# Twenty more warm-up products, wider buffers in a ring of weights, and the low parts of all weights on VectorE

## The chip, the core and the metric

The kernel runs on one core of a Trainium2 chip. The core has a matrix engine (TensorE, PE in the rows, with its weight loads as PEld), a vector engine (VectorE, DVE), an activation engine (ScalarE, ACT), a general engine (GpSimd, POOL) and a queue engine that issues most transfers (SyncE, SP). They run side by side and wait for one another through semaphores. The metric is the device time of one execution in microseconds; the time of a kernel is the median of its runs.

## What is computed

One decoder block on a sequence of 1024 tokens of width 1024, all in float32. A conditioning vector gives shift, scale and gate; a combined input projection feeds a pooling mixer and a chunked state-space (SSD) mixer; an output projection and a squared-ReLU MLP follow:

```python
mod = einsum('bd,de->be', silu(c), w_ada) + b_ada          # six vectors: shift, scale, gate, twice
u = rms_norm(h, g_mix) * (1 + scale_m) + shift_m
proj = einsum('bsd,de->bse', u, w_in)                      # pool | z | x,B,C | dt
y_pool = pool_mixer(proj[..., :OFF_Z], w_pool, pool_scale)
y_ssd = ssd_mixer(z, u_xbc, u_dt, ...)                     # causal conv, silu, chunked scan, gate by silu(z), norm
h = h + gate_m * einsum('bse,ed->bsd', concat(y_pool, y_ssd), w_out)
u = rms_norm(h, g_mlp) * (1 + scale_f) + shift_f
f = square(relu(einsum('bsd,df->bsf', u, w_up)))
h = h + gate_f * einsum('bsf,fd->bsd', f, w_down)
return rms_norm(h, g_final)
```

## The kernel before

Each large product of two float32 matrices is done as three products of a reduced 32-bit format (fp32r): an operand is split into a high part `hi`, a rounded copy made by ScalarE (line 195), and a low part `lo`, which is operand minus `hi` (line 196). `mm3` (line 238) then issues hi·hi, hi·lo and lo·hi on TensorE; line 245 is its one matmul, so nearly all matmuls of the profile have that line.

The work comes in stages. Stage 1, the start: x is loaded, normalized by rows, transposed on TensorE (line 139) and scaled by the first shift and scale vectors, which are themselves products of the conditioning vector with pieces of `w_ada` (partly on VectorE, lines 441 to 443 and 265 to 267, partly on TensorE, lines 450, 368, 370 and 464). Eight steps (`chunk`, line 483) then accumulate six 128x512 results. Until the first step can begin, `busy(n)` (line 332) issues plain float32 products whose result nobody reads: 7 after the first transpose, and 2 at a time between the early pieces of work. In this stage the order on ScalarE, VectorE, GpSimd and TensorE is the written one (`pinned`). Stage 2 (about 72 to 330 us): the other columns of the input projection. `feat` (line 601) makes 128 channels for 512 tokens with 24 matmuls; `conv_half` (line 551) takes the result through a copy to `craw` (ACT), a small copy of three columns (POOL, lines 558, 560), one activation (line 562), three multiply-adds on VectorE (line 565), a tanh (line 568) and a last multiply (line 573 or 576); a transpose of the result on TensorE follows 12 us of planned time later (line 583). The short `dec` steps on VectorE (lines 641 to 653) turn the step sizes dt of the scan, and the scan itself is mixed in. Stage 3 (to 540 us): the z columns, the norm, and the output projection `gemm2` (line 967), where the weights are the moving operand. Stage 4 (to the end): the MLP, whose operands lie in other buffers (`dhi`, `dlo`, `whl`).

Weights of stages 2 and 3, and of the first products of the MLP, pass through a ring: `unit` (line 184) loads a piece to `raw`, and splits it to `hi` and `lo`. The ring's six `hi` and six `lo` buffers have 544 floats, that is 2176 bytes a partition, and lie one behind the other. In the built program the six `hi` buffers begin at bytes 203200, 205376, 207552 and so on, the `lo` buffers at 216256, 218432 and so on: by turns 192 and 64 bytes past a multiple of 256. The pieces take the buffers in turn. The other operands of the matmuls (`u`, `ym`, `dhi`, `dlo`, `whl`) all begin 192 past such a multiple. The ring of stage 1 has 768 floats a buffer.

`ring["pool_lo"]` says which engine makes `lo`: GpSimd for the 15 pieces asked for between line 529 and line 780, VectorE for all others. Outside the pinned stage the order of each engine's instructions is set by the framework's scheduler from the program and its own costs. `z_tok` (line 884) gates with z: a tanh to `th`, a product to `sz`, a product to `tok`.

Of the kernel before, what the change touches and what calls it, by code (L numbers as in the profile page):

```python
# [9 lines left out]
F32 = mybir.dt.float32  # L10
F32R = mybir.dt.float32r
BF16 = mybir.dt.bfloat16
AF = mybir.ActivationFunctionType
ALU = mybir.AluOpType
# [3 lines left out]
P = 128  # L18
# [16 lines left out]
NFG = DFF // HW  # L35
EPS = 1e-5
UM = 544
WARM = 7
CUTS = (0, 0, 0, 2, 4, 4, 0)
TDVE = (1, 2, 3)  # L40
AP = (4, 1, 1, 1, 1, 1, 1)
# [29 lines left out]
def tile_hybrid_block(  # L71
# [112 lines left out]
    def unit(kn, ncol, parts, gate=None):  # L184
        n = kn * ncol
        rp, hp, w, rb, hb = ring["now"]
        raw = rp.tile([P, w], F32, name="raw", tag="raw" if w == UM else "raws", bufs=rb)
        rv = raw[:, :n].rearrange("p (k c) -> p k c", c=ncol)
        for c0, c1, src in parts:
            sp.dma_start(out=rv[:, :, c0:c1], in_=src)  # L190
        if gate is not None:
            dve.tensor_tensor(out=rv, in0=rv, in1=gate.unsqueeze(1).broadcast_to([P, kn, ncol]), op=ALU.mult)
        hi = hp.tile([P, w], F32R, name="hi", tag="hi", bufs=hb)
        lo = hp.tile([P, w], F32R, name="lo", tag="lo", bufs=hb)
        act.copy(hi[:, :n], raw[:, :n])  # L195
        (pool if ring.get("pool_lo") else dve).tensor_tensor(  # L196
            out=lo[:, :n], in0=raw[:, :n], in1=hi[:, :n].bitcast(F32), op=ALU.subtract)
        hv = hi[:, :n].rearrange("p (k c) -> p k c", c=ncol)
        lv = lo[:, :n].rearrange("p (k c) -> p k c", c=ncol)
        return [(hv[:, k, :], lv[:, k, :]) for k in range(kn)]  # L200
# [118 lines left out]
    def row_rs(t, eng=dve):  # L319
        square_sum(t, slice(0, D), t, utmp().bitcast(BF16))  # L320
        rsqrt_cols(t, t + 1, D, eng)
# [9 lines left out]

    def busy(n):
        for _ in range(n):
            pe.matmul(warm_ps[:, 0:P], lhsT=ident, rhs=ones, start=True, stop=True)  # L334

    def transpose_x(k, h, ps):
        for i in range(4):
# [68 lines left out]
    ring["now"] = (stp, stp, 768, 2, 2)  # L406
    kw = []
    with pinned((act, dve, pool, pe)):
        row_rs(0)
        row_scale(0, False)  # L410
        row_rs(1)
        pst = bank()
        turn(pst[:, 0:P], pr0[:, :])
        busy(WARM)
        dve.tensor_copy(out=pc[:, 0:64], in_=pst[:, 0:64])
        dve.tensor_scalar(out=chf, in0=pc[:, 0:8], scalar1=0.5, scalar2=None, op0=ALU.mult)
        row_scale(1, False)
        row_rs(2)
        act.activation(out=cth, in_=pc[:, 0:8], func=AF.Tanh, scale=0.5)
        dve.scalar_tensor_tensor(out=cact, in0=cth, scalar=1.0, in1=chf, op0=ALU.add, op1=ALU.mult)  # L420
        for j in (8, 32):
            sl = pc[:, C_BADA + j:C_BADA + j + 8]
            dve.tensor_scalar(out=sl, in0=sl, scalar1=1.0, scalar2=None, op0=ALU.add)
        row_scale(2, False, slice(0, HW))
        row_rs(3)
        row_scale(2, True, slice(HW, D))
        spec = specs.popleft()
        raw0 = stp.tile([P, 768], F32, name="raw", tag="raws", bufs=2)
        for c0, c1, src in spec[2]:
            sp.dma_start(out=raw0[:, c0:c1].unsqueeze(1), in_=src)  # L430
        ada_load(0)
        acc = [stp.tile([P, 256], F32, name="adaa", tag="adaa", bufs=4)[:, :P] for _ in range(2)]
        hi0 = stp.tile([P, 768], F32R, name="hi", tag="hi", bufs=2)
        lo0 = stp.tile([P, 768], F32R, name="lo", tag="lo", bufs=2)

        def dve_f0(ks):
            for k in ks:
                a = acc[k % 2]
                src = ada_w[0][:, k, 0:P]
                if k < 2:  # L440
                    dve.tensor_scalar(out=a, in0=src, scalar1=cact[:, k:k + 1], scalar2=None, op0=ALU.mult)
                else:
                    dve.scalar_tensor_tensor(out=a, in0=src, scalar=cact[:, k:k + 1], in1=a,
                                             op0=ALU.mult, op1=ALU.add)

        pa, pb = bank()[:, 0:1], bank()[:, 0:1]

        def pe_f1(ks):
            for k in ks:
                pe.matmul(pb, lhsT=ada_w[0][:, k, P:2 * P], rhs=cact[:, k:k + 1], start=k == 0, stop=k == KD - 1)  # L450

        act.copy(hi0, raw0)
        dve_f0(range(2))
        row_scale(3, False, slice(0, HW))
        row_scale(3, True, slice(HW, D))
        dve_f0(range(2, KD))
        dve.tensor_tensor(out=lo0, in0=raw0, in1=hi0.bitcast(F32), op=ALU.subtract)
        for i in range(3):
            pe_f1(range(2 * i, 2 * i + 2))
            busy(2)  # L460
        stage_x(0)
        pe_f1(range(6, KD))
        for i in range(2):
            pe.matmul(pa, lhsT=acc[i], rhs=ones[:, 0:1], start=i == 0, stop=i == 1)
        ada_cols(0, pa, pb)
        ada_u(0)
        stage_x(1)
        busy(WARM2)
        kw.append([(hi0, lo0)])
        ada_load(1)  # L470
        pool.dma_start(out=pr1[0:48, :], in_=conv_w[0].rearrange("k (r p) -> (k r) p", p=P))
        pool.dma_start(out=pr1[48:60, :], in_=rows(conv_b))
        pool.dma_start(out=pr1[64:72, :], in_=rows(g_mlp))
        pool.dma_start(out=pr1[72:80, :], in_=rows(g_ssd))
        pool.dma_start(out=pr1[80:84, :], in_=rows(pool_scale))
        pool.dma_start(out=dtb, in_=dt_bias.broadcast_to([P, HEADS]))
        pool.dma_start(out=nea, in_=a_log.broadcast_to([P, HEADS]))
        pool.dma_start(out=dsk, in_=d_skip.broadcast_to([P, HEADS]))
# [4 lines left out]
    def chunk(k):  # L483
# [22 lines left out]
            kw.append(get(1, 0))  # L506
        if k == 5:
            ring["now"] = (unitm, unitm, UM, 4, 6)
            ring["pool_lo"] = False
            for i in range(4):  # L510
                specs.append((2, 256, [
                    (0, Z0, win_r[:, 2 * i:2 * i + 2, OFF_Z:OFF_Z + Z0]),
                    (Z0, 256, win_r[:, 2 * i:2 * i + 2, OFF_DT:OFF_DT + HEADS])], None))
            feat_specs(G1[0][0])
            prefetch(NPF)
# [10 lines left out]
    chunk(6)  # L526
    chunk(7)
    prefetch(6)
    ring["pool_lo"] = True
    st.close()  # L530
    for off, _ in G0 + G1[1:]:
        feat_specs(off)
# [244 lines left out]
    for _, ct in G0:  # L777
        conv_half(ct, 1, feat(get(2, 3), 1))
        step(5.2)
    ring["pool_lo"] = False  # L780
    queue_ssd(0)
    for i, (_, ct) in enumerate(G1[1:]):
        ks = get(2, 3)
# [100 lines left out]
    def z_tok(si, t, ks):  # L884
# [3 lines left out]
        tok_mm(ps[:, :n], t, ks)  # L888
        th = accp.tile([P, 272], F32, name="zt", tag="zt", bufs=2)
        act.activation(out=th[:, :n], in_=ps[:, :n], func=AF.Tanh, scale=0.5)  # L890
        sz = accp.tile([P, 272], F32, name="sz", tag="sz", bufs=2)
        dve.scalar_tensor_tensor(out=sz[:, :n], in0=th[:, :n], scalar=1.0, in1=ps[:, :n],
                                 op0=ALU.add, op1=ALU.mult)
        dve.scalar_tensor_tensor(out=tok[:, t, a:b], in0=tok[:, t, a:b], scalar=0.5, in1=sz[:, :n],
                                 op0=ALU.mult, op1=ALU.mult)
        if si != 1:
            g = 0 if si == 0 else 1
# [652 lines left out]
```

## Time and profile before

| | |
|---|---|
| median of 3 runs | 1170.3 us (1166.7 to 1172.98) |
| the profiled execution | 1170.18 us |
| its span, first to last instruction | 1168.3 us |
| busy: PE, DVE, ACT, POOL | 1143.4 (98%), 823.9 (71%), 561.8 (48%), 169.7 us (15%) |
| 15 `lo` on POOL, mean | 1.46 us each, 100.4 to 147.5 us |
| mean granted TensorE clock | 0.997 of 2.4 GHz |

TensorE is busy nearly all the span, so time is lost where it waits, where it runs at its lower clock, or where one product takes longer than another of the same size. A matmul's row shows its own duration, which overlaps the next; the rate is read from the distance between starts. The clock column has no record before the first change of the clock, and shows 1.00 there; the durations tell which level it was. A float32 product appears as two matmul records, an fp32r product or a transpose as one.

### The profile page before, as it was taken

Reading aid. Unit: us, or ns where it says so; the run is one execution under the profiler, and the core shown is the slowest. Engines: PE = TensorE matmul, PEld = TensorE weight load, DVE = VectorE, ACT = ScalarE, POOL = GpSimd, SP = SyncE. Lnnn points to the kernel's source line nnn. Section 1 sums busy time; section 2 is a strip of 40 time slices with the busy share of each in tenths; the row PEclk is TensorE's granted clock in tenths of the full one; section 3 lists DMA queues with packets and bytes.
Section 4 is the critical chain, followed back from the end, with each engine's and each line's share of the span. In section 5 each row is a group of like instructions: output and inputs, shape, how many; then the busy total and the mean of one; then the engine's idle time right before and its main releaser. Section 6 shows DMA issues by size and latency. Waiting matters only on the chain.

```text
span 1168.3 us, 15472 instructions
## 1 busy us (share of the span) xinstructions
PE 1143.4 (98%) x5639; PEld 953.8 (82%) x5639; DVE 823.9 (71%) x1220; ACT 561.8 (48%) x981; POOL 169.7 (15%) x204
## 2 busy tenths in 40 slices
PE   7999999999999999999999999999999999999997
PEld 6888787777799888887778888888888888888885
DVE  3878789967978656664888666665567844586985
ACT  4476575544434633534764444444354344334373
POOL 3014436514500011122000000000100000000030
PEclk9999999999999999999999999999999999999999
DMA  9942233233367646753166434351499934775732
GB/s 260 241 137 61 68 129 106 72 86 114 100 197 226 205 140 201 259 162 126 37 212 220 151 147 170 128 189 72 154 399 358 320 110 144 238 262 186 270 127 90
DMA packets 124908, 200.73 MB, mean 172 GB/s; under 512 B 8448, under 2 KB 67616, under 8 KB 122784
## 3 DMA queue, kind: packets, MB, share of 16 engines
q1 hardware_dynamic: 123472, 196.24, 50.3%
q0 software_dynamic: 1120, 3.21, 0.8%
q8 instruction: 44, 0.72, 0.3%
q14 instruction: 32, 0.26, 0.1%
q10 hardware_dynamic: 240, 0.30, 0.1%
HBM read 159.81 MB, written 39.91 MB: 171 GB/s over the span
## 4 chain that ended last, share of the span: by engine, by line
PE 83%; DVE 8%; DMA 3%; ACT 3%; issue 2%; POOL 1%; POOLq 0%; SPq 0%; ACTq 0%; DVEq 0%
PE bank L245 74%; PE bank L743 2%; DMA raw<-in_w_ada_dram 2%; DVE cv L565 2%; PE bank L139 2%; PE bank L747 1%; PE bank L740 1%; DVE acc L851 1%; PE bank L334 1%; PE bank L819 1%; DVE lo L196 1%; ACT tok L905 1%; PE bank L1026 1%; POOL rst L180 0%; DMA adaa<-in_b_ada_dram 0%
## 5 line engine op out<-in xcount | busy, mean ns | idle before, releaser
L245 PE MATMUL bank<-u,hi 128*128 128x512 f32 x560 | 185.6, 411 | 0.4 <-ACT u L386 0.4
L245 PE MATMUL bank<-dhi 128*128 128x512 f32 (+1 forms) x452 | 175.1, 387 | 1.1 <-DVE tmp L1446 1.1
L245 PE MATMUL bank<-dlo,dhi 128*128 128x512 f32 (+1 forms) x452 | 175.0, 387 | 0.0
L245 PE MATMUL bank<-dhi,dlo 128*128 128x512 f32 (+1 forms) x452 | 175.0, 387 | 0.0
L1380 ACT CAST dhi<-fr 128x1024 fp32r<-128x1024 f32 x56 | 59.0, 1054 | 144.4 <-PE bank L245 110.5
L245 PEld LDWEIGHTS bank<-u,hi 128*128 128x128 f32 x560 | 104.6, 191 | 28.0 <-issue 5.0
L1381 DVE TENSOR_TENSOR dlo<-fr,dhi 128x1024 fp32r<-128x1024 f32 x56 | 68.5, 1224 | 83.3 <-ACT dhi L1380 83.0
L245 PE MATMUL bank<-hi,ym 128*128 128x512 f32 x384 | 125.4, 400 | 0.0
L195 ACT CAST hi<-raw 128x512 fp32r<-128x512 f32 (+2 forms) x109 | 67.9, 633 | 90.8 <-PE bank L245 70.1
L245 PE MATMUL bank<-u,lo 128*128 128x512 f32 x280 | 111.1, 397 | 0.0
L196 DVE TENSOR_TENSOR lo<-raw,hi 128x512 fp32r<-128x512 f32 (+2 forms) x94 | 72.2, 781 | 48.5 <-ACT hi L195 48.1
L245 PEld LDWEIGHTS bank<-dhi 128*128 128x128 f32 x452 | 84.9, 188 | 18.5 <-DVE tmp L1446 1.3
L245 PEld LDWEIGHTS bank<-dlo,dhi 128*128 128x128 f32 x452 | 84.9, 188 | 17.5
L245 PEld LDWEIGHTS bank<-dhi,dlo 128*128 128x128 f32 x452 | 84.9, 188 | 17.3
L245 PE MATMUL bank<-hi,u 128*128 128x256 f32 (+1 forms) x512 | 97.4, 288 | 0.2
L245 PE MATMUL bank<-E,whl 128*128 128x512 f32 x384 | 91.6, 389 | 0.0
L245 PEld LDWEIGHTS bank<-hi,ym 128*128 128x128 f32 x384 | 72.1, 188 | 16.4 <-issue 0.7
L180 POOL TENSOR_TENSOR rst<-ssq,mhalf 128x1 f32<-128x1 f32 (+2 forms) x27 | 26.9, 998 | 400.9 <-DVE ssq L179 375.8
L245 PEld LDWEIGHTS bank<-E,whl 128*128 128x128 f32 x384 | 72.1, 188 | 15.0
L245 PEld LDWEIGHTS bank<-hi,u 128*128 128x128 f32 x512 | 80.1, 189 | 1.4 <-issue 0.7
L245 PE MATMUL bank<-u,whl 128*128 128x512 f32 x312 | 75.2, 389 | 0.8 <-ACT whl L1160 0.8
L245 PE MATMUL bank<-lo,ym 128*128 128x512 f32 x192 | 75.4, 392 | 0.0
(257 smaller groups left out, 2144.6 us busy)
## 6 DMA issues: line engine op xcount, KB each, us to landing
f_d<-tok SPq DMA_DIRECT2D x16, 1792.0 KB, 7.3
wr<-in_w_down_dram SPq DMA_DIRECT2D x56, 512.0 KB, 5.0
fr<-f_d SPq DMA_DIRECT2D x53, 512.0 KB, 4.4
raw<-in_w_ada_dram SPq DMA_DIRECT2D x64, 256.0 KB, 3.1
wraw<-in_w_up_dram SPq DMA_DIRECT2D x16, 1024.0 KB, 5.4
raw<-in_w_in_dram SPq DMA_DIRECT2D x48, 256.0 KB, 3.0
raw<-in_w_out_dram SPq DMA_DIRECT2D x48, 256.0 KB, 2.8
tok<-in_x_dram SPq DMA_DIRECT2D x16, 512.0 KB, 6.1
```

Source lines behind the costliest of these rows:

```text
L139: return pe.transpose(dst, src, ident)
L180: pool.tensor_tensor(out=rst[:, a:b], in0=m, in1=mhalf[:, :b - a], op=ALU.pow)
L195: act.copy(hi[:, :n], raw[:, :n])
L196: (pool if ring.get("pool_lo") else dve).tensor_tensor(out=lo[:, :n], in0=raw[:, :n], in1=hi[:, :n].bitcast(F32), op=ALU.subtract)
L245: pe.matmul(ps, lhsT=st_, rhs=mv, start=first and i == 0, stop=last and i == 2, skip_group_check=more)
L334: pe.matmul(warm_ps[:, 0:P], lhsT=ident, rhs=ones, start=True, stop=True)
L565: dve.scalar_tensor_tensor(out=v, in0=cr[:, k:k + HW], scalar=pw[:, 12 * k + ct:12 * k + ct + 1], in1=v, op0=ALU.mult, op1=ALU.add)
L740: pe.matmul(po, lhsT=C[:, cs], rhs=states[g], start=True, stop=True)
L743: pe.matmul(py[:, hh * HD:(hh + 1) * HD], lhsT=Ms[hh // 4][:, (hh % 4) * P:(hh % 4 + 1) * P], rhs=xdt[:, hh * HD:(hh + 1) * HD], start=Tru ...
L747: pe.matmul(pst_, lhsT=btok, rhs=xw, start=True, stop=True)
L1380: act.copy(hi, src)
L1381: dve.tensor_tensor(out=lo, in0=src, in1=hi.bitcast(F32), op=ALU.subtract)
```

## The change

Twenty products are issued ahead of the first transpose. The products of `busy` take `ones` as both operands, where one was `ident` before (`ident` is made on GpSimd, `ones` by a memset on VectorE). The ring's `hi` and `lo` buffers get 576 floats (2304 bytes, 9 times 256) of which as many are used as before; in the built program all twelve then begin 192 past a multiple of 256. All `lo` are made on VectorE. `z_tok` overwrites `th` in place of using `sz`; the bytes of the two `sz` buffers go to the ring.

```diff
+UP = 576
 WARM = 7
+WARM0 = 20
...
-        hi = hp.tile([P, w], F32R, name="hi", tag="hi", bufs=hb)
-        lo = hp.tile([P, w], F32R, name="lo", tag="lo", bufs=hb)
+        hi = hp.tile([P, UP if w == UM else w], F32R, name="hi", tag="hi", bufs=hb)
+        lo = hp.tile([P, UP if w == UM else w], F32R, name="lo", tag="lo", bufs=hb)
         act.copy(hi[:, :n], raw[:, :n])
-        (pool if ring.get("pool_lo") else dve).tensor_tensor(
-            out=lo[:, :n], in0=raw[:, :n], in1=hi[:, :n].bitcast(F32), op=ALU.subtract)
+        dve.tensor_tensor(out=lo[:, :n], in0=raw[:, :n], in1=hi[:, :n].bitcast(F32), op=ALU.subtract)
...
-            pe.matmul(warm_ps[:, 0:P], lhsT=ident, rhs=ones, start=True, stop=True)
+            pe.matmul(warm_ps[:, 0:P], lhsT=ones, rhs=ones, start=True, stop=True)
...
     with pinned((act, dve, pool, pe)):
+        busy(WARM0)
         row_rs(0)
...
-            ring["pool_lo"] = False
...
-    ring["pool_lo"] = True
...
-    ring["pool_lo"] = False
...
-        sz = accp.tile([P, 272], F32, name="sz", tag="sz", bufs=2)
-        dve.scalar_tensor_tensor(out=sz[:, :n], in0=th[:, :n], scalar=1.0, in1=ps[:, :n],
+        dve.scalar_tensor_tensor(out=th[:, :n], in0=th[:, :n], scalar=1.0, in1=ps[:, :n],
                                  op0=ALU.add, op1=ALU.mult)
-        dve.scalar_tensor_tensor(out=tok[:, t, a:b], in0=tok[:, t, a:b], scalar=0.5, in1=sz[:, :n],
+        dve.scalar_tensor_tensor(out=tok[:, t, a:b], in0=tok[:, t, a:b], scalar=0.5, in1=th[:, :n],
```

The first rows of TensorE before. L139 is the first transpose, of the small parameters; L334 the products of `busy`; L450 the first shift products.

```order
L139 MATMUL bank<-ident,adaa 128x128
L334 MATMUL bank<-ones,ident 128x128 x7
L450 MATMUL bank<-cact,adaw 128x1 x2
L334 MATMUL bank<-ones,ident 128x128 x2
L450 MATMUL bank<-cact,adaw 128x1 x2
```

The same place after (lines have moved by one or two: L335 is `busy`, L141 the transpose).

```order
L335 MATMUL bank<-ones 128x128 x20
L141 MATMUL bank<-ident,adaa 128x128
L335 MATMUL bank<-ones 128x128 x7
L452 MATMUL bank<-cact,adaw 128x1 x2
L335 MATMUL bank<-ones 128x128 x2
L452 MATMUL bank<-cact,adaw 128x1 x2
```

The transpose stands behind the twenty; the rest of TensorE's order is the same to the end.

GpSimd in stage 2 before, from the last carry of the first half of a convolution on. L196 is a `lo`, L560 the small copy that a convolution's second half needs.

```order
L560 COPY craw<-car 128x3
L196 TENSOR_TENSOR lo<-raw,hi 128x512 x2
L560 COPY craw<-carry_782 128x3
L196 TENSOR_TENSOR lo<-raw,hi 128x512 x2
L560 COPY craw<-carry_783 128x3
L196 TENSOR_TENSOR lo<-raw,hi 128x512
L560 COPY craw<-carry_784 128x3
```

The same place after.

```order
L560 COPY craw<-car 128x3
L560 COPY craw<-carry_802 128x3
L560 COPY craw<-carry_803 128x3
L560 COPY craw<-carry_804 128x3
L560 COPY craw<-carry_805 128x3
```

No `lo` is left there.

VectorE in stage 2 before, up to the last multiply (L576, `cv_1449`) of the sixth of these convolutions, whose transpose follows on TensorE. L565 are multiply-adds of a convolution, L573 its last multiply where B or C channels are made, L698 a product of the scan, `bt` and `ct` are B and C.

```order
L573 SCALAR_TENSOR_TENSOR bt_835<-craw_1334,cv_1337 128x512
L698 TENSOR_TENSOR xdt_1742<-tok_66,dt_795 128x512
L698 TENSOR_TENSOR xdt_1819<-tok_66,dt_795 128x512
L565 SCALAR_TENSOR_TENSOR cv_1396<-craw_1393,pw_117,cv_1396 128x512 x3
L573 SCALAR_TENSOR_TENSOR ct_876<-craw_1393,cv_1396 128x512
L565 SCALAR_TENSOR_TENSOR cv_1449<-craw_1446,pw_117,cv_1449 128x512 x3
L576 SCALAR_TENSOR_TENSOR cv_1449<-craw_1446,cv_1449 128x512
```

The same place after (L198 is a `lo`; `cv_1469` is the tile that was `cv_1449`).

```order
L565 SCALAR_TENSOR_TENSOR cv_1416<-craw_1413,pw_117,cv_1416 128x512
L198 TENSOR_TENSOR lo_1485<-raw_1482,hi_1484 128x512
L198 TENSOR_TENSOR lo_1540<-raw_1537,hi_1539 128x512
L573 SCALAR_TENSOR_TENSOR ct_896<-craw_1413,cv_1416 128x512
L698 TENSOR_TENSOR xdt_1762<-tok_66,dt_815 128x512
L565 SCALAR_TENSOR_TENSOR cv_1469<-craw_1466,pw_117,cv_1469 128x512
L198 TENSOR_TENSOR lo_1546<-raw_1543,hi_1545 128x512
L565 SCALAR_TENSOR_TENSOR cv_1469<-craw_1466,pw_117,cv_1469 128x512
L698 TENSOR_TENSOR xdt_1839<-tok_66,dt_815 128x512
L565 SCALAR_TENSOR_TENSOR cv_1469<-craw_1466,pw_117,cv_1469 128x512
L198 TENSOR_TENSOR lo_1593<-raw_1590,hi_1592 128x512
L576 SCALAR_TENSOR_TENSOR cv_1469<-craw_1466,cv_1469 128x512
```

Four `lo` stand in these rows where none stood, between the last steps of two convolutions, and the two L698 are apart. Of the 15 `lo`, 14 stand ahead of this L576.

## Rows read from the trace of the kernel before

**Rows 1.** The page: busy time, share of the span and instructions of TensorE, and the chain that ended last by line.

```profile
PE 1143.4 (98%) x5639; PEld 953.8 (82%) x5639; DVE 823.9 (71%) x1220; ACT 561.8 (48%) x981; POOL 169.7 (15%) x204
...
PE bank L245 74%; PE bank L743 2%; DMA raw<-in_w_ada_dram 2%; DVE cv L565 2%; PE bank L139 2%; PE bank L747 1%; PE bank L740 1%; DVE acc L851 1%; PE bank L334 1%; PE bank L819 1%; DVE lo L196 1%; ACT tok L905 1%; PE bank L1026 1%; POOL rst L180 0%; DMA adaa<-in_b_ada_dram 0%
```

**Rows 2.** TensorE's timeline of the start. Columns: start us, us that the group takes, engine, line, operation, out<-in, count, and in brackets the idle time before it with its releaser. A plain float32 product counts as two.

```profile
7.64 0.45 PE L139 MATMUL bank<-ident,adaa 128*128 128x128 f32 x1 [7.64 <-DMA adaa<-in_b_ada_dram]
7.88 3.19 PE L334 MATMUL bank<-ones,ident 128*128 128x128 f32 x14
...
16.04 1.06 PE L139 MATMUL bank<-ident,tok 128*128 128x128 f32 x4
...
20.06 0.77 PE L245 MATMUL bank<-u,hi 128*128 128x512 f32 x1
...
22.31 0.39 PE L245 MATMUL bank<-u,lo 128*128 128x512 f32 x1
22.54 0.39 PE L245 MATMUL bank<-u,hi 128*128 128x512 f32 x1
...
28.77 0.60 PE L139 MATMUL bank<-ident,tok 128*128 128x128 f32 x4
```

**Rows 3.** The timeline of the start, VectorE (DVE) and SyncE's queue of transfers (SPq), same columns.

```profile
0.91 0.17 DVE L142 MEMSET ones<- 128x128 f32 x1 [0.91 <-PEq L1536]
...
13.00 0.61 DVE L443 SCALAR_TENSOR_TENSOR adaa<-adaw,cact,adaa 128x128 f32<-128x128 f32 x2 [0.29 <-DMA adaw<-in_w_ada_dram]
...
13.53 0.95 DVE L457 TENSOR_TENSOR lo<-raw,hi 128x768 fp32r<-128x768 f32 x1
...
28.03 0.95 DVE L196 TENSOR_TENSOR lo<-raw,hi 128x768 fp32r<-128x768 f32 x1
...
29.01 1.35 SPq L190 DMA_DIRECT2D raw<-in_w_in_dram  x3
```

**Rows 4.** Stretches of the start. Columns: from:to, length, then busy us and count of PE, PEld, DVE, ACT, POOL, then the granted clock, the DMA share, GB/s.

```profile
20.00:22.00 2.00, 2.00 (x9) 1.72 (x9) 1.49 (x4) 0.58 (x2) 0.00 (x0) 1.00 1.17 293
...
26.00:28.00 2.00, 2.00 (x15) 1.84 (x15) 0.71 (x3) 0.44 (x1) 0.00 (x0) 1.00 0.09 21
28.00:30.00 2.00, 2.00 (x16) 1.69 (x15) 2.00 (x5) 0.97 (x3) 0.00 (x0) 1.00 0.02 5
```

**Rows 5.** TensorE's timeline in stage 2, columns as in rows 2.

```profile
140.48 0.66 PE L139 MATMUL bank<-ident,cv 128*128 128x128 f32 x4 [2.71 <-DVE cv L576]
...
142.90 1.06 PE L245 MATMUL bank<-u,hi 128*128 128x512 f32 x2
143.76 0.63 PE L245 MATMUL bank<-u,lo 128*128 128x512 f32 x1
```

**Rows 6.** The stretch behind that wait, columns as in rows 4.

```profile
140.50:145.00 4.50, 4.50 (x15) 3.66 (x16) 3.19 (x4) 2.16 (x8) 3.54 (x4) 0.64 0.27 73
```

**Rows 7.** Groups of instructions by line and shape: the first three VectorE from 96 to 139.7 us, the fourth GpSimd in the same stretch, the last VectorE from 60 to 90 us. Columns: line, engine, operation, names, shapes, count | busy us, mean ns of one | idle us before them.

```profile
L565 DVE SCALAR_TENSOR_TENSOR cv<-craw,pw,cv 128x512 f32<-128x512 f32 x23 | 22.6, 1001 | 1.4 <-ACT cv L562 1.2
L576 DVE SCALAR_TENSOR_TENSOR cv<-craw,cv 128x512 f32<-128x512 f32 x4 | 4.0, 1011 | 0.5 <-ACT craw L568 0.5
L649 DVE SCALAR_TENSOR_TENSOR dec<-dec 128x128 f32<-128x128 f32 x8 | 3.4, 423 | 0.1
...
L196 POOL TENSOR_TENSOR lo<-raw,hi 128x512 fp32r<-128x512 f32 x13 | 18.8, 1445 | 4.0 <-ACT hi L195 4.0
...
L196 DVE TENSOR_TENSOR lo<-raw,hi 128x512 fp32r<-128x512 f32 x6 | 3.9, 687 | 2.5 <-ACT hi L195 2.5
```

**Rows 8.** The same three lines of VectorE over the whole span: shortest/median/longest in ns, first and last start.

```profile
L565 DVE SCALAR_TENSOR_TENSOR cv<-craw,pw,cv x72: 736/750/1848, 74.5 to 238.7; 128x512 f32<-128x512 f32 x72
...
L576 DVE SCALAR_TENSOR_TENSOR cv<-craw,cv x16: 679/692/1465, 99.1 to 240.2; 128x512 f32<-128x512 f32 x16
...
L649 DVE SCALAR_TENSOR_TENSOR dec<-dec x8: 279/292/1371, 112.6 to 118.1; 128x128 f32<-128x128 f32 x8
```

**Rows 9.** VectorE's timeline in stage 2, columns as in rows 2.

```profile
127.70 1.66 DVE L698 TENSOR_TENSOR xdt<-tok,dt 128x512 f32<-128x512 f32 x2 [0.79 <-ACT tok L582]
...
133.68 0.69 DVE L573 SCALAR_TENSOR_TENSOR ct<-craw,cv 128x512 f32<-128x512 f32 x1 [1.04 <-ACT craw L568]
135.59 3.39 DVE L565 SCALAR_TENSOR_TENSOR cv<-craw,pw,cv 128x512 f32<-128x512 f32 x3 [1.22 <-ACT cv L562]
139.73 0.69 DVE L576 SCALAR_TENSOR_TENSOR cv<-craw,cv 128x512 f32<-128x512 f32 x1 [0.76 <-ACT craw L568]
...
146.23 1.78 DVE L196 TENSOR_TENSOR lo<-raw,hi 128x512 fp32r<-128x512 f32 x1
```

**Rows 10.** The chain of waits in order of time: start us, us, engine, line, count.

```profile
154.84 5.57 PE bank L245 x24
...
594.16 562.65 PE bank L245 x2481
```

**Rows 11.** TensorE's timeline in stage 3, columns as in rows 2.

```profile
414.12 0.39 PE L245 MATMUL bank<-lo,ym 128*128 128x512 f32 x1
...
414.80 0.39 PE L245 MATMUL bank<-lo,ym 128*128 128x512 f32 x1
...
416.86 0.40 PE L245 MATMUL bank<-lo,ym 128*128 128x512 f32 x1
...
417.56 0.39 PE L245 MATMUL bank<-lo,ym 128*128 128x512 f32 x1
```

## The prediction

> **What bounds the kernel now.** I read the page's busy shares first: TensorE is busy 98% of the span, and one line, L245, is 74% of the chain that ended last [rows 1]. The reader is to see that nothing can be won in general by a faster VectorE or GpSimd; only three things count: when TensorE's real work begins, where TensorE idles, and how long one product takes. So I went on with TensorE's timeline at the start, then its longest wait in stage 2, then the distance between starts of like products.
>
> At the start TensorE runs at its lower level of 1.2 GHz although the clock column shows 1.00 there: four transposes take 1.06 us at 16.04 and 0.60 at 28.77, and products follow each other at 0.23 us only from 22.31 on [rows 2]. The first product of the projection starts at 20.06 [rows 2]. Transfers set the pace up to about 26 us (share 1.17 at 20 to 22), then nearly nothing moves for some 4.5 us (0.09 and 0.02) [rows 4], because SP's loads for a later step, issued at 29.01, wait for a buffer that VectorE's `lo` of 28.03 sets free [rows 3].
>
> In stage 2 TensorE stands still for 2.71 us ahead of a transpose at 140.48 that needs VectorE's L576, and after it the clock falls: products 0.43 us apart (142.90 to 143.76, two of them) [rows 5], mean granted clock 0.64 in 140.5 to 145 [rows 6]. At 0.64 of full speed 4.5 us hold 4.5 x 0.64 = 2.9 us of work, so the low stretch costs 1.6 us. Stall and fall together: 2.7 + 1.6 = 4.3 us.
>
> **Part A, the twenty products.** Each is a plain float32 product, two records. The seven of before are 14 records in 3.19 us at half rate [rows 2], 0.228 us each; 40 records take 9.1 us if the clock stays low. They need only `ones`, which is there at 0.91 + 0.17 [rows 3], so they run from about 1.2 to at most 10.3 us, in a time in which TensorE waited for the parameters until 7.64 [rows 2]. If the clock rises on the way, halfway say, they are through at about 7.6 and delay nothing; if it never does, the first transpose is 10.3 - 7.6 = 2.7 us late. What a warm TensorE gives: the small products of 8 to 20 us take half as long, and TensorE is no longer what the first step waits for. Late next is VectorE: its last L443 ends at 13.6 and its `lo` L457 at 14.5 [rows 3]; with about 1.6 us for the scaling behind it (estimated from the spacing of such pieces) the first product could start near 16.1 in place of 20.06, 4.0 earlier. The 2.25 us from 20.06 to 22.31 at half rate become 1.1: together 5.1 us earlier. All this pulls TensorE's use of the weights forward, while the transfers up to 26 us are full and can't come earlier; what gives way is the 4.5 us hole behind them [rows 4]. I take the smaller: **-4.5**; ends: -5.1, and +2.7 for a late transpose with no rise at all.
>
> **Part B, the `lo` of stage 2.** From 96 to 139.7 us GpSimd makes 13 of them in 18.8 us, and VectorE's operations beside them are long [rows 7]: against the medians of the whole span [rows 8] L565 has 23 x (1001 - 750) = 5.8 us too much, L576 4 x (1011 - 692) = 1.3, L649 8 x (423 - 292) = 1.0. That is 8.1 us, which should go when GpSimd reads nothing there. What comes: 14 `lo` ahead of the L576 that TensorE waits for; six alone on VectorE took 3.9 us [rows 7], 0.65 each, so 14 x 0.65 = 9.1. The two nearly cancel: added 1.0. But VectorE idles 0.79 + 1.04 + 1.22 + 0.76 = 3.8 us ahead of that L576, each time for ScalarE [rows 9], and the scheduler has put `lo` and the second L698 into those places. L576 ended at 139.73 + 0.69 = 140.4; it now ends between 140.4 + 1.0 = 141.4 (nothing fits into the waits) and 141.4 - 3.8 = 137.6 (all does). TensorE gets there at 140.48 - 2.71 = 137.8. I take the filled end, because the order of the program shows the `lo` there; then the wait goes and the clock doesn't fall: **-4.3**; ends: -4.3 and, with 1.0 more wait, +1.0. Behind L576 on VectorE stand the multiply-adds of the next convolution; they lose what one `lo` in their midst takes, and TensorE's transposes come 12 us of plan later, which covers it. What GpSimd keeps are the small copies (L560), which then no longer stand behind a 1.4 us `lo`.
>
> The Trainium skill ("SBUF — State Buffer", section "Who interferes with whom") says that a VectorE instruction with two inputs in the state buffer contends with a GpSimd instruction that reads it. The trace agrees: 1001 against 750 ns for L565. The same section says that TensorE never waits on anyone; by that rule part C is worth nothing, and the total is 4.0 less gain (rival 3).
>
> **Part C, the buffers of the ring.** In the MLP, where all operands begin 192 bytes past a multiple of 256, 2481 products take 562.65 us: 226.8 ns each. A convolution's 24 products from the ring take 5.57: 232 ns [rows 10]. In stage 3 the step of three products is 0.68 us at 414.12 with a buffer of the one kind, 0.70 at 416.86 with the other [rows 11]: 233 against 227, 6.7 ns per product. That it is the address is my reading; the two differ in nothing else that I can see. 512-column products from this ring: 26 x 24 in stage 2, 48 x 12 in stage 3, 72 at the start of the MLP, 1272; in half of the first two kinds the buffer lies at 64: 50 dozens x 12 x 6.7 ns = **-4.0**. Ends: zero, and 1272 x (232 - 226.8) = -6.6 (a stretch seems to need a while to settle: the whole convolution shows 232 though only half of it lies at 64).
>
> **The rest.** `busy` with `ones` twice costs what it did. Without `sz` the next tanh into `th` waits for one more VectorE product, half a microsecond of an engine that is 71% busy, against 98% for TensorE [rows 1]; nothing. SP's order does not change.
>
> **Sum**, against the profiled execution (1170.18 us, of which 1168.3 span and 1.9 around it; the median is 1170.3, so they may be taken as one): 1170.2 - 4.5 - 4.3 - 4.0 = 1157.4, forecast 1157.
>
> **Rivals.**
> 1. *The clock doesn't hold at the start.* The small products of 10 to 20 us leave TensorE idle once they run twice as fast, and the clock may be low again when the projection begins. For it: TensorE was busy from 7.64 to 22.31 without reaching the higher level [rows 2]. Against it: twenty products in a row are denser than anything in that stretch. Then part A gives between nothing and -3: 1170.2 - 8.3 = 1162 to 1159. The Trainium skill ("TensorE: Matmul & The Clock Gate", section "Part 1: The HAM clock gate") says that the low level is the default, that activity releases it, and that how many products run slow differs from run to run; the first agrees with rows 2, the last no run here shows.
> 2. *VectorE becomes the bound in stage 2.* The waits don't fill, L576 ends at 140.4 to 141.4, the clock falls all the same: part B between 0 and +1: 1170.2 - 8.5 = 1161.7 to 1162.7, 1162. For it: 137.6 against 137.8 is close, and by parts A and C TensorE arrives earlier still.
> 3. *The address does nothing*: the 6.7 ns come of something else, such as the stretch's neighbours. 1170.2 - 8.8 = 1161.4. For it: the 232 of a whole convolution.
> 4. *Slower: VectorE's `lo` are stretched themselves.* One of before, beside a GpSimd `lo`, took 1.78 us [rows 9]. If the long durations of 96 to 140 come from transfers or from ScalarE and not from GpSimd, they stay, and 14 `lo` at 1.78 add 24.9 less 3.8 of waits = 21.1 us ahead of L576. All of it is TensorE's wait: 1170.2 + 21.1 - 8.5 = 1183. It decides from 14 x d - 3.8 > 8.5, d = 0.88 us, on. Against it: the 0.65 us of the six between 60 and 90 us, with the same transfers about.
> 5. *Two parts fail together*: 1164 to 1166.
>
> **How the numbers follow.** Forecast 0.50, with its own range 1154 to 1160 (A and C at their ends); rival 1 0.21, rival 2 0.13, rival 3 0.08, rival 4 0.04, rival 5 0.04. The range 1152.5 to 1164.5 holds the first four cases and the ends of A and C (-5.1 - 4.3 - 6.6 gives 1154) but not the last two. Half a per cent, about what a measurement of this kernel can tell from no change, is 5.9 us: faster means under 1164.4. Forecast and rivals 1 to 3 lie below it, 0.92, of which I take off 0.07 for costs that I don't see: 0.85. Same 0.11 (rival 5 and that 0.07), slower 0.04 (rival 4).
>
> **What would show it.** A: four transposes near 13 to 16 us at 0.60 in place of 1.06, the first L245 near 16, a shorter hole in the transfers behind 26 us, the end of stage 1 some 4.5 us earlier. B: L565 near 750 ns, `lo` near 0.65 on VectorE, no idle TensorE of over 0.5 us ahead of the transposes, no stretch with a granted clock of 0.64. C: 24 products of a convolution in 5.44 to 5.5 us in place of 5.57, stage 3 without steps of 0.70. The forecast is wrong if the first transpose comes after 10 us, if the wait for L576 is still over 1 us, or if a convolution still takes 5.57.

## The result, and the profile after

The changed kernel takes 1160.8 us (median of 16 executions, 1157.7 to 1166.9) against 1170.4 of the kernel before on the same chip (16 executions, 1165.1 to 1177.8): ratio 0.9926, 95% interval 0.9905 to 0.9948. That is 0.5 to 1% faster, inside the range on record, and 3.8 us above the forecast of 1157. The profiled execution took 1157.7 us, span 1156.0: of 1168.3 - 1156.0 = 12.3 us the forecast had 12.8. Those two statements don't fit together at once, and the larger part of the experiments is about why.

The start. TensorE's timeline of the profiled execution, columns as in [rows 2]:

```profile
1.13 7.62 PE L335 MATMUL bank<-ones 128*128 128x128 f32 x40 [1.13 <-DVE ones L144]
8.59 0.27 PE L141 MATMUL bank<-ident,adaa 128*128 128x128 f32 x1
8.69 1.73 PE L335 MATMUL bank<-ones 128*128 128x128 f32 x14
...
13.45 0.60 PE L141 MATMUL bank<-ident,tok 128*128 128x128 f32 x4
...
16.12 0.51 PE L246 MATMUL bank<-u,hi 128*128 128x512 f32 x1 [0.34 <-ACT u L254]
```

The twenty run in 7.6 us and end at about 8.7; the seven behind them take 1.73 us and not 3.19, the four transposes 0.60 and not 1.06, and the first product of the projection starts at 16.12 and not at 20.06, now waiting for ScalarE. The transfers have no hole left (columns as in [rows 4]):

```profile
26.00:28.00 2.00, 2.00 (x14) 1.68 (x12) 0.85 (x1) 0.00 (x0) 0.00 (x0) 1.00 0.99 281
28.00:30.00 2.00, 2.00 (x16) 1.88 (x16) 0.56 (x3) 0.22 (x1) 0.00 (x0) 1.00 1.13 307
```

Stage 2. VectorE's groups from 90 to 127 us, nearly the same work as in [rows 7]:

```profile
L565 DVE SCALAR_TENSOR_TENSOR cv<-craw,pw,cv 128x512 f32<-128x512 f32 x24 | 17.8, 740 | 0.1
L198 DVE TENSOR_TENSOR lo<-raw,hi 128x512 fp32r<-128x512 f32 x14 | 9.5, 681 | 0.0
L576 DVE SCALAR_TENSOR_TENSOR cv<-craw,cv 128x512 f32<-128x512 f32 x4 | 2.7, 684 | 0.0
L649 DVE SCALAR_TENSOR_TENSOR dec<-dec 128x128 f32<-128x128 f32 x8 | 2.3, 281 | 0.0
```

L565 is at 740 ns in place of 1001, L576 at 684 in place of 1011, L649 at 281 in place of 423, and fourteen `lo` stand among them without idle time. The transposes of the sixth convolution, which waited 2.71 us [rows 5], follow the products ahead of them without a bracket; TensorE's timeline there:

```profile
131.91 0.39 PE L246 MATMUL bank<-u,lo 128*128 128x512 f32 x1
132.15 0.60 PE L141 MATMUL bank<-ident,cv 128*128 128x128 f32 x4
```

No stretch of 3 us up to 570 us, and none in the MLP, has a granted clock under 0.995, where [rows 6] had 0.64. The products, from the chain of waits (columns as in [rows 10]):

```profile
74.50 2.87 PE bank L246 x24
...
138.76 5.48 PE bank L246 x24
...
398.71 21.81 PE bank L246 x96
...
581.82 562.67 PE bank L246 x2481
```

A convolution takes 5.48 us where it took 5.57. The MLP's row is the same to 0.02 us, and it starts at 581.82 in place of 594.16 [rows 10]: all 12.3 us are won ahead of it.

### The profile page after: what moved, and what is told of

It reads as the page before. It is cut to its first block, busy times and chain, and to the rows that moved or that the text cites. A ratio compares the mean times of both kernels' runs of the same rounds, so it can differ in the third digit from the quotient of the medians.

```text
span 1156.0 us, 15542 instructions
## 1 busy us (share of the span) xinstructions
PE 1139.4 (99%) x5679; PEld 953.3 (82%) x5679; DVE 822.0 (71%) x1235; ACT 562.8 (49%) x981; POOL 150.0 (13%) x189
## 3 DMA queue, kind: packets, MB, share of 16 engines
q0 software_dynamic: 1120, 3.21, 0.8%
## 4 chain that ended last, share of the span: by engine, by line
PE 87%; DVE 5%; DMA 3%; ACT 2%; issue 2%; POOL 1%; SPq 0%; POOLq 0%; DVEq 0%; ACTq 0%
PE bank L246 78%; PE bank L743 2%; DMA raw<-in_w_out_dram 2%; PE bank L141 2%; DVE lo L198 1%; PE bank L747 1%; PE bank L740 1%; PE bank L335 1%; PE bank L818 1%; DMA tok<-in_x_dram 0%; DVE adaa L268 0%; POOL rst L182 0%; POOL tok L974 0%; DMA raw<-ypool_d 0%; ACT hi L197 0%
## 5 line engine op out<-in xcount | busy, mean ns | idle before, releaser
L246 PE MATMUL bank<-u,hi 128*128 128x512 f32 x560 | 182.0, 404 | 0.7 <-ACT u L387 0.4
L198 DVE TENSOR_TENSOR lo<-raw,hi 128x512 fp32r<-128x512 f32 (+2 forms) x109 | 83.1, 775 | 47.0 <-ACT hi L197 46.4
```

The source lines that it names most:

```text
L198: dve.tensor_tensor(out=lo[:, :n], in0=raw[:, :n], in1=hi[:, :n].bitcast(F32), op=ALU.subtract)
L246: pe.matmul(ps, lhsT=st_, rhs=mv, start=first and i == 0, stop=last and i == 2, skip_group_check=more)
```

## The experiments

The single parts first, each alone in the kernel before.

**The twenty products alone.**

```diff
...
-            pe.matmul(warm_ps[:, 0:P], lhsT=ident, rhs=ones, start=True, stop=True)
+            pe.matmul(warm_ps[:, 0:P], lhsT=ones, rhs=ones, start=True, stop=True)
...
+        busy(WARM0)
         row_rs(0)
```

> The kernel before with the twenty products ahead of the first transpose (and ones as both operands) as its only edit. My theory: the first product of the projection starts near 16.1 us in place of 20.1, stage 1 ends 4.5 to 5 us earlier, and the time falls by 4.5 us; stage 2 keeps its wait for L576 and the ring its 232 ns. Rival (the clock doesn't hold): the start is won in some executions only, and the median falls by 0 to 3 us.

Measured: median 1168.0 against 1170.1, ratio 0.9991, interval 0.9972 to 1.0009: the medians lie 2.1 us apart, but the interval does not tell this from nothing. (The one execution with a trace took 1265.7 us at a granted clock of 0.85, so part A alone has no trace here that could be compared.) But the single times say more than the median. Four of the other eleven lie at 1165.1 to 1166.1 with a mean clock of 0.997 or 0.998; seven at 1167.5 to 1173.0, with 0.989 to 0.995. The kernel before had 28 such times in the same session: nine at 1165.3 to 1166.3, with 0.997 or 0.998, and thirteen at 1169.6 to 1171.4, with 0.996 to 0.998. So the lower group is no lower with the twenty products than without them; they do away with the group at 1170.6 and bring executions with a lower clock in its place.

**All `lo` on VectorE alone.**

```diff
-        (pool if ring.get("pool_lo") else dve).tensor_tensor(
+        dve.tensor_tensor(
```

> The kernel before with all low parts on VectorE as its only edit. My theory: L565 at 750 ns between 96 and 140 us, no wait of over 0.5 us ahead of the transposes, no low clock behind it, time lower by 4.3 us. Rival (VectorE becomes the bound): a wait of 2 to 3 us for L576 stays, and the time moves by less than 1 us.

Measured: 1165.2, ratio 0.9973, interval 0.9954 to 0.9991. VectorE's groups from 85 to 133 us, and from TensorE's timeline the transposes in question, without a wait:

```profile
L565 DVE SCALAR_TENSOR_TENSOR cv<-craw,pw,cv 128x512 f32<-128x512 f32 x27 | 20.0, 742 | 0.1
L196 DVE TENSOR_TENSOR lo<-raw,hi 128x512 fp32r<-128x512 f32 x14 | 9.5, 684 | 0.2 <-ACT hi L195 0.2
```
```profile
137.72 0.60 PE L139 MATMUL bank<-ident,cv 128*128 128x128 f32 x4
```

Here too there are two groups: four times at 1161.1 to 1162.4, and four at 1166.3 to 1167.5 with a clock of 0.996 or more. Each is some 4 us under the group of before that it answers to (1165.9, 1170.6). The stretch of VectorE's operations came from GpSimd's `lo` and went with them; rival 2 falls.

**The ring alone** (576 floats a buffer, `z_tok` without `sz`).

```diff
-        hi = hp.tile([P, w], F32R, name="hi", tag="hi", bufs=hb)
+        hi = hp.tile([P, UP if w == UM else w], F32R, name="hi", tag="hi", bufs=hb)
...
-        sz = accp.tile([P, 272], F32, name="sz", tag="sz", bufs=2)
```

> The kernel before with the ring's buffers of 576 floats (and z_tok without sz, which pays for them) as its only edit. My theory: 24 products of a convolution take 5.48 us in place of 5.57, stage 3 has no steps of 0.70, the time falls by 3 to 4 us. Rival (the address does nothing): 5.57 stays and the time is that of before.

Measured: 1167.3, ratio 0.9984, interval 0.9965 to 1.0002, which alone would settle nothing. The groups do: one time at 1162.6, seven at 1166.9 to 1167.9, 3.3 us under 1165.9 and 1170.6. From its chain a convolution, and from TensorE's timeline the wait that is still there:

```profile
148.79 5.48 PE bank L246 x24
```
```profile
140.52 0.66 PE L140 MATMUL bank<-ident,cv 128*128 128x128 f32 x4 [3.21 <-DVE cv L577]
```

**The changed kernel again**, in the same session.

> The changed kernel once more. If its executions differ because the clock is low for a stretch in some of them, an execution of 1160 us or more shows one or two stretches of low granted clock that the profile of 1157.7 us did not have, of 1.7 us cost each or so, and the rest of its timeline is the same. If they differ for another reason (transfers), the clock is full and a wait is longer. As a sum of the three single edits it should lie 4.5 + 4.3 + 3 = 12 us under the kernel before when the clock holds.

Measured: 1159.8, ratio 0.9924, interval 0.9906 to 0.9941; three times at 1158.4 to 1158.8 (clock 0.997 or 0.998), three at 1160.8 to 1161.7 (0.994 or 0.995). The profiled execution fell into the first group (1158.75). Its clock holds through the start, but it falls late, from 581.5 to 584.9 us, where TensorE has just waited for operands of the MLP (stretches, columns as in [rows 4]):

```profile
582.00:584.00 2.00, 2.00 (x6) 1.56 (x5) 2.00 (x4) 1.82 (x4) 0.00 (x0) 0.50 0.90 280
584.00:586.00 2.00, 2.00 (x8) 1.60 (x8) 1.38 (x3) 0.60 (x2) 0.00 (x0) 0.78 0.62 213
```

The 22 products there take 6.88 us; in the profile after, whose clock held, they take 5.29 (TensorE's timeline, of this execution, then of the profile after):

```profile
581.22 6.88 PE L246 MATMUL bank<-A,whl 128*128 128x512 f32 x22 [0.47 <-DVE whl L1163]
```
```profile
581.82 5.29 PE L246 MATMUL bank<-A,whl 128*128 128x512 f32 x22 [0.58 <-DVE whl L1163]
```

So a second place costs 1.6 us in some executions, although the wait ahead of it is there in both. The traces of e6, e7, e8 and e9 below have the same fall between 581 and 590 us, and that of b2 has one at 601 to 604; the traces of the kernel before, of the profile after and of e2, e3, e5, b1 and e10 have none there. The group at 1160.8 to 1161.7 stayed open here.

**The address itself.** The changed kernel with all ring buffers used from the 32nd float on, and with the 16th.

```diff
-        hi = hp.tile([P, UP if w == UM else w], F32R, name="hi", tag="hi", bufs=hb)
+        hi = hp.tile([P, UP if w == UM else w], F32R, name="hi", tag="hi", bufs=hb)[:, OFF if w == UM else 0:]
```

> The changed kernel with every hi and lo of the ring used from its 32nd float on, so that all twelve begin 64 bytes past a multiple of 256 (u and ym stay at 192). If the residue 64 is what costs, every dozen is slow: 24 products of a convolution take 5.57 to 5.6 us, stage 3 steps of 0.70 all through, and the time is 4 to 6 us above the changed kernel. Rival: it is the change of residue from one buffer to the next that costs, not the residue itself; then a convolution keeps 5.48 us and the time stays.

> The same with the 16th float, all twelve at a multiple of 256 itself. If only operands at the same residue as the others (192) are fast, this is as slow as 64: 5.57 us for a convolution. If a buffer that begins on a multiple of 256 is at least as good as 192, it stays at 5.48 and the time at that of the changed kernel.

Measured: 1164.4 (ratio 0.9959, 0.9942 to 0.9975) and 1164.6 (0.9965, 0.9947 to 0.9983). At the same mean clock that is 3.7 us over the changed kernel for 64 (1162.0 against 1158.3 at 0.998) and 3.2 for 0 (1164.0 against 1160.8 at 0.994 to 0.995). The trace at 64 and the profile after, both without a fall of the clock, have spans of 1160.3 and 1156.0 us, 4.3 apart. The trace at 0 has two falls (13.2 to 20.0 and 586.6 to 590.1 us), so only its single products are compared. The chain at 64, then at 0; the first row of each is a convolution, the others are stage 3:

```profile
152.21 5.59 PE bank L247 x24
...
401.76 22.30 PE bank L247 x96
424.50 2.80 PE bank L247 x12
```
```profile
154.81 5.60 PE bank L247 x24
...
403.91 21.99 PE bank L247 x96
426.33 2.76 PE bank L247 x12
```

All twelve buffers now have the same place past a multiple of 256, and every dozen is slow at 64, so it is the place itself, not the alternation. The other operands lay at 192 in every kernel here: whether 192 is good by itself, or because both operands of a product then begin at the same place, no run tells apart. And the two roles differ: in a convolution, where the ring holds the stationary operand, 0 is as bad as 64 (5.60); in stage 3, where it holds the moving one, 0 lies between (21.99, against 21.81 at 192 and 22.30 at 64).

**The changed kernel without the twenty products.**

> The changed kernel without the twenty products. My theory after the single edits: the start of the kernel before comes in two forms in different executions, a slow one (first product of the projection at 20 us) and a fast one some 4.8 us shorter, and the twenty products make the fast one certain; so times here fall into two groups, near 1158.4 and near 1163.2, few in between, and the median is 0 to 4 us above the changed kernel. Rival: the start is always the slow one, all times near 1163.

Measured: 1163.3, ratio 0.9949, interval 0.9934 to 0.9965; all six times at 1163.2 to 1163.7. The upper group lies where it was expected, the lower one did not come. Of 80 executions of the kernel before in all sessions (one of 4 ms left out) 24 were under 1167; with such a share six in a row miss it one time in eight, so six times don't decide whether it is gone here. The trace shows the slow start (first product at 20.05 us), and the late fall of the clock besides (585.6 to 589.0 us).

**More products where the start is thin.**

```diff
-            busy(2)
+            busy(4)
...
-        busy(WARM2)
+        busy(2 * WARM2)
```

> The changed kernel with 4 products in place of 2 at the four later places in the start. Theory: the times of 1160.7 and more come from a clock that falls back between 10 and 16 us, where TensorE has little to do; with more products there it holds, nearly all executions lie at 1158 to 1159 with a mean clock of 0.997 or more, or up to 1.5 us above where the products themselves delay the start. Rival: the clock falls elsewhere (later, in the first steps), and the times still spread from 1158 to 1167.

Measured: 1161.5, ratio 0.9941, interval 0.9921 to 0.9961, times from 1159.6 to 1169.8: the rival is right. In the profiled execution (1161.5) the clock held from 12 to 23.7 us; the first product came late (17.66), and the clock fell behind it, where the shift products of the next step give TensorE one column at a time (stretches, columns as in [rows 4]):

```profile
22.00:24.00 2.00, 2.00 (x17) 2.00 (x17) 0.22 (x2) 0.00 (x0) 0.00 (x0) 0.92 1.04 321
24.00:26.00 2.00, 2.00 (x6) 1.52 (x6) 1.89 (x4) 0.82 (x1) 0.00 (x0) 0.50 1.11 286
```

It fell a second time late, from 583.5 to 586.9 us.

**The kernel before, two more executions.**

> The kernel before, unchanged, for the trace of one more execution. Its times fall into two groups, near 1165.8 and near 1170.6, at the same mean clock. Theory: in the faster group TensorE's clock is up before the first step, the first product of the projection starts near 16 us and not at 20, and from there on all is the same 4.8 us earlier, the wait for L576 and the low clock behind it included. Rival: the groups differ elsewhere (the wait in stage 2 is there in one and not in the other). An execution of 1170 us says nothing new.

The first took 1164.8 us, an execution of the lower group, and shows what the first profile could not. TensorE's timeline, start and stage 2:

```profile
12.00 0.69 PE L334 MATMUL bank<-ones,ident 128*128 128x128 f32 x4
...
13.42 0.60 PE L139 MATMUL bank<-ident,tok 128*128 128x128 f32 x4
...
16.10 0.50 PE L245 MATMUL bank<-u,hi 128*128 128x512 f32 x1 [0.34 <-ACT u L253]
```
```profile
135.54 0.66 PE L139 MATMUL bank<-ident,cv 128*128 128x128 f32 x4 [2.73 <-DVE cv L576]
```

Without any product ahead of the first transpose, the first product of the projection starts at 16.10: the same start as the changed kernel's. The wait for L576 is there as before, 4.94 us earlier than in [rows 5]. The second execution:

> The kernel before once more, with the same expectation as the run ahead of it.

It took 1177.6 us: the slow start, and behind it a clock that falls back once more, from 27.4 to 37.7 us (stretches, columns as in [rows 4]), and again from 600.9 to 604.3 us:

```profile
28.00:30.00 2.00, 2.00 (x6) 1.67 (x7) 1.51 (x4) 0.82 (x1) 0.00 (x0) 0.50 0.00 0
30.00:32.00 2.00, 2.00 (x8) 1.55 (x7) 2.00 (x6) 0.00 (x0) 0.00 (x0) 0.50 0.26 63
```

**Fewer products in the same gaps, and a fill of the second.**

```diff
-            busy(2)
+            busy(3)
...
+                if k == 1:
+                    pe.matmul(warm_ps[:, 0:P], lhsT=ada_a[k][i][:, fs], rhs=ones, start=True, stop=True)
```

> The changed kernel with 3 products in place of 2 at the three early places, and one 128-column product behind each of the four shift products of ada_pe(1), where TensorE has next to nothing to do for 2.6 us at 19.5. Theory: the clock falls back in the two thin places of the start (13 to 20 us and 22 to 27 us); with both filled it holds in most executions, which then lie near 1159 to 1159.5 (the fill itself costs up to 1 us), and the group of 1160.7 to 1167 gets small. Rival: the fill delays the start as in the kernel with 4 products, and the median stays at 1161 or more.

Measured: 1161.2, ratio 0.9931, interval 0.9905 to 0.9957; two times at 1158.0 and 1159.4, four at 1161.2 to 1162.5 with a clock of 0.994 to 0.996. No gain over the changed kernel: in its profiled execution (1159.4) the clock held through the start, but the first product started at 16.95, and the clock fell late, from 581.5 to 584.9 us, as in e4. Where it fell in the four with a mean clock of 0.994 to 0.996, no trace here shows.

**The changed kernel, one more execution.**

> The changed kernel, unchanged, for the trace of one more execution. Theory: in the executions of 1160.4 us and more the clock falls back in the thin places of the start, between 13 and 28 us, as the kernel with buffers at multiples of 256 showed at 13 to 20 us; the first product of the projection then starts near 18 us, the end of stage 1 is 2.5 us later, and behind it all is the same. Rival: the clock is full up to 30 us and falls later, in stage 2 or 3. An execution of 1158 us says nothing new.

Measured: 1160.3 us, by its time at the lower edge of the group that the median stands for; its mean clock of 0.996 is a little above the 0.994 or 0.995 of that group. The stretches with their clock (columns as in [rows 4]), then the first product in TensorE's timeline, then a row of the chain:

```profile
10.00:12.00 2.00, 1.26 (x12) 1.29 (x12) 1.58 (x6) 1.86 (x3) 1.34 (x4) 1.00 1.16 291
12.00:14.00 2.00, 2.00 (x14) 2.00 (x15) 2.00 (x7) 0.21 (x1) 2.00 (x5) 0.71 1.15 292
14.00:16.00 2.00, 2.00 (x12) 2.00 (x10) 0.37 (x1) 0.58 (x1) 1.66 (x4) 0.50 1.16 285
...
18.00:20.00 2.00, 2.00 (x10) 1.77 (x9) 1.53 (x4) 0.57 (x2) 0.00 (x0) 0.58 1.14 292
```
```profile
18.11 0.78 PE L246 MATMUL bank<-u,hi 128*128 128x512 f32 x1
```
```profile
77.19 2.87 PE bank L246 x24
```

The clock is at its lower level from 12.8 to some 19.7 us; the first product starts 2.0 us later than at 16.12, runs at half rate for its first 1.6 us, and at 77.19 against 74.50 the execution is 2.7 us behind. Behind that nothing differs by more than 0.1 us (1160.3 - 1157.7 = 2.6), and the MLP begins without a fall.

Just before the fall TensorE had been idle for 0.90 us. But in e4, whose clock held there, it idled still longer at the same place, 1.26 us, so that idle time alone does not say when the clock falls (TensorE's timeline, of this execution, then of e4):

```profile
10.74 0.58 PE L452 MATMUL bank<-cact,adaw 128*128 128x1 f32 x4 [0.90 <-DVE ssq L181]
```
```profile
10.72 0.58 PE L452 MATMUL bank<-cact,adaw 128*128 128x1 f32 x4 [1.26 <-DMA adaw<-in_w_ada_dram]
```

## Why the prediction came out as it did

The direction and the three mechanisms were right; the sum of 12.8 us stands against 12.3 in the profiled execution, and the forecast is 3.8 us below the median. That the median lies in the range all the same is owed to the range's width; it lies where rival 1 put it.

*Part A, forecast -4.5.* From 79.37, the row in the chain of before for the same 24 products,

```profile
79.37 2.86 PE bank L245 x24
```

to 74.50 it is -4.9: the first product at 16.1, the four transposes at 0.60 and the closed hole in the transfers came as said. What failed is the step that takes this term from one profiled execution to the median, "they may be taken as one". 24 of 80 executions of before are short enough to have started as fast without any of the products; one of them is traced, and there the part is worth nothing (b1 beside the profile after: 16.10 and 16.12). And the changed kernel pays something new: in 17 of its 23 executions (16, 6 and the last execution) the time is 1160.3 or more. The one of these with a trace shows the clock fallen from 12.8 us on, in the thin stretch between the twenty products and the projection, at a cost of 2.7 us. So in this execution, against the common one of before, the term is -4.9 + 2.7 = -2.2. The medians agree with such a size: alone the part is 2.1 us (1168.0 against 1170.1, inside the interval of no change), and the changed kernel without it is 2.5 slower (1163.3 against 1160.8, in another session). How the other sixteen lost their time is not shown: another trace of the changed kernel lost 1.6 us in the MLP instead (e4), which the prediction did not have at all. The fall at the start is rival 1, to which I gave 0.21 and 1159 to 1162; the median of 1160.8 lies in it, and the forecast case is the lower quarter of the executions (6 of 23, 1157.7 to 1158.8). The trace of before carried the warning: it showed a clock that doesn't rise under steady small products, which was named there and weighed too low. The sentence of the Trainium skill cited with that rival ("TensorE: Matmul & The Clock Gate", section "Part 1: The HAM clock gate"), that how many products run slow differs from run to run, now has its runs: the transposes at 1.06 us in the first trace of before and at 0.60 in the second.

*Part B, forecast -4.3.* Right in amount: with `lo` alone on VectorE each group fell by some 4 us, and between the two traces the lead grows from 137.77 - 132.15 = 5.6 us, where TensorE arrives at these transposes (140.48 - 2.71 before), to 10.0 behind the low stretch (the same two products at 145.33 and 135.32). The size of the margin was wrong, on the safe side. From the multiply of the last B channels to the end of L576 it took 95.36 to 140.42 before, 90.39 to 128.11 after (VectorE's timeline, of before and of after):

```profile
95.36 0.69 DVE L573 SCALAR_TENSOR_TENSOR bt<-craw,cv 128x512 f32<-128x512 f32 x1
```
```profile
90.39 0.68 DVE L573 SCALAR_TENSOR_TENSOR bt<-craw,cv 128x512 f32<-128x512 f32 x1
...
127.42 0.69 DVE L576 SCALAR_TENSOR_TENSOR cv<-craw,cv 128x512 f32<-128x512 f32 x1 [0.27 <-ACT craw L568]
```

That is 45.1 and 37.7 us, 7.3 less in spite of fourteen `lo` more. I had 140.4 - 137.6 = 2.8 less. L576 is done 4.0 us ahead of its transposes at 132.15, not 0.2, and rival 2 was never near. VectorE's idle time in this stretch went from 4.9 to 0.8 us, 4.2 less, near the 3.8 forecast; what was wrong is its busy time, 3.2 us less (40.15 and 36.96) where I had 1.0 more. Stretched operations that I had left out are part of this, such as one L650 at 1266 ns before and 282 after; the rest is not worked out.

*Part C, forecast -4.0.* 12.3 - 4.9 - 4.3 = 3.1 us are left for it in the profiled execution, and the groups of the ring alone give 3.3. That the two agree is luck, since each is a larger gain less a wait. The convolutions give 26 x (5.57 - 5.48) = 2.3, where the forecast had 26 x 12 x 6.7 ns = 2.1: right. For stage 3 it had 24 x 12 x 6.7 ns = 1.9. In a long run that holds, 0.30 for 96 products in a row (22.11 against 21.81), but a dozen between two transposes gains half of it. From the first of these rows to the second, of before and then of after, lie five such dozens in 16.08 and 15.99 us, 0.02 each and not 0.04 (the first row shown is the one of 96):

```profile
410.57 22.11 PE bank L245 x96
433.12 2.79 PE bank L245 x12
449.20 2.77 PE bank L245 x12
```
```profile
420.96 2.78 PE bank L246 x12
436.95 2.76 PE bank L246 x12
```

By the distance of like products in the traces, stage 3 gives 1.6 us in the ring alone and in e4. In the profile after 0.8 of that is lost again, at three pairs of products near 492 us that take 0.97, 0.92 and 0.86 us where before took 0.63; by the profile TensorE waits there for VectorE and ScalarE (after, then the same products before):

```profile
491.82 0.97 PE L246 MATMUL bank<-hi,ym 128*128 128x512 f32 x2
```
```profile
504.68 0.63 PE L245 MATMUL bank<-hi,ym 128*128 128x512 f32 x2
```

In the ring alone the loss is elsewhere: TensorE arrives earlier at the wait for L576, which grows to 3.21 us from 2.71. Rival 3 falls with the all-64 kernel: the address decides. The rule of the Trainium skill weighed there ("SBUF — State Buffer", section "Who interferes with whom", TensorE never waits on anyone) was taken in the prediction to make the part nothing. The runs decide otherwise, with 5.59 against 5.48 us from the buffers' place alone; the rule is about engines that get in each other's way, which is not what made this difference.

*Rival 4* fell: fourteen `lo` at 681 ns, far under the 0.88 from which it would have decided. It needed a stretch that doesn't come from GpSimd, and `lo` alone on VectorE showed that it does. *Rival 5* fell too: each of the three parts shows in the profile after.

The sum closes: 1170.6 (common group of before) - 4.9 - 4.3 - 3.3 = 1158.1, the lower group after; and 1165.9 - 4.3 - 3.3 = 1158.3 from the other start. With the 2.7 us of a fallen clock it is 1160.8, as the median, but the 2.7 come from one traced execution, and the late fall of 1.6 us and the wait of 0.8 are not in this sum. What stays open is which falls the common execution of the changed kernel has, what decides them, and how a start could be filled that keeps the clock up without delaying the first product: both attempts moved the fall or paid for it, and no version here was faster than the changed kernel.

## What to carry to other kernels

Before a term is priced from one profile, look at the list of single times: two groups 5 us apart at one mean clock are two kernels, and a gain worked out from a trace of one of them can be none in the other. Warming TensorE early helps only where the clock then stays up; where it fell again behind the twenty products, 2.7 of the 4.9 us were given back. Follow the clock's row to the end of the trace before calling an execution free of falls: here one stands at 581 us, behind half of the kernel. Where a product's rate differs between stages with the same operands, compare where the buffers begin before looking for waits.

## What was not expected of the hardware

- The same program starts in two ways: with TensorE at its higher level by 11 us (24 of 80 executions of before by their times, one of them traced) or at the lower one until 22 us or later, 4.9 us apart, and the clock column shows 1.00 for both.
- Where a matmul's operand begins in memory changes its rate: 226.8 to 228 ns for 512 columns with all operands 192 bytes past a multiple of 256, 232 to 233 with the ring's at 64; at 0 the stationary operand is as slow as at 64, the moving one in between. All other operands were at 192. Why is not shown by any run.
- TensorE's clock fell back while the engine's row of busy time was full: in e8 at 23.7 us, with 2.00 of 2.00 us busy in each stretch from 12 to 24 us. And it held in e4 behind 1.26 us of idle time at 10 us, where in e10 it fell behind 0.90. Neither a full row nor a short gap told which way it went.
